# Attention: who subtracts the low parts of the weights, and who scales the softmax

## The chip, the cores and the metric

The kernel runs on one core of a Trainium2 chip. The metric is the device time of one execution in microseconds (us). The core has TensorE for matmuls and transposes (PE in the rows, and PEld for its loads of the stationary operand), VectorE (DVE), ScalarE (ACT), GpSimd (POOL) and SyncE (SP), which issues most of the DMA transfers. Each engine works through its own instructions in order and waits on semaphores for the others.

## The reference

A trunk of two layers over 512 positions of width 1024: sliding-window attention, a feed-forward network, a gated DeltaNet, and a second feed-forward network. Only the attention is touched. It projects to 16 query heads and 4 key and value heads of 64 dimensions, normalises and rotates queries and keys, and takes for each block of 128 queries a softmax over this and the previous block of keys, with a learned sink:

```python
qkv = u @ w_in
q = partial_rope(rms_norm(q, q_gain), cos, sin)
k = partial_rope(rms_norm(k, k_gain), cos, sin)
scores = jnp.einsum("bnqhgd,bnkhd->bnhgqk", qb, kb) * (hd ** -0.5)
scores = jnp.where(mask[None, :, None, None], scores, jnp.finfo(jnp.float32).min)
probs = jax.nn.softmax(jnp.concatenate([scores, sink], axis=-1), axis=-1)[..., :-1]
out = jnp.einsum("bnhgqk,bnkhd->bnqhgd", probs.astype(vb.dtype), vb)
return out.reshape(B, S, ATTN_Q_DIM) @ w_out
```

## The kernel before

Every large matmul is made of three: a float32 operand is split into a high part, rounded to the type that TensorE takes fast, and a low part, the rest. `mm3` (lines 146 to 150) multiplies high by high, high by low and low by high into the same accumulator. `weight` (line 128) prepares a weight tile: SyncE loads `raw` (line 136), ScalarE casts it to `whi` (line 137), VectorE subtracts to `wlo` (line 138). The three tiles have three buffers each, so a tile's cast has to wait until TensorE is through with the tile three before it.

The attention (`attn`) has three parts that run into each other.

- The projection is six blocks, c = 0 to 5, of 256 columns: keys, two blocks of queries, values, two blocks of queries. A block uses two weight tiles of 128x1024, one for k = 0 to 3 and one for k = 4 to 7, each k taking 256 of the 1024 columns. From c = 1 on, the loop runs over four position blocks t outside and over k inside, three matmuls for each. In the projection the high part of the input is the first operand, so of the three matmuls line 148 and line 150 read `whi`, and line 149 reads `wlo`. After each block `post` normalises and rotates (`qk_norm`, a long series of small VectorE instructions that contains the Newton steps of `rsqrt`, lines 163 to 169), ScalarE and VectorE each copy half of the keys to `kd` (line 420), and TensorE transposes them.
- Two lanes, i = 0 and 1, take two key heads each through the softmax. `attn_scores` forms the scores of four query heads (line 515), VectorE adds the mask and takes the maximum (line 518), ScalarE forms the exponentials and their sums (line 524), VectorE takes the reciprocal (line 526), and line 528 scales the four: heads 0 and 2 on VectorE, 1 and 3 on GpSimd. `attn_turn` transposes the scaled weights on TensorE (line 537) and copies them back (`pT`, line 539), and `attn_values` multiplies by the values (line 546). There are 16 such softmaxes, of 128 columns for the first block of a lane and of 256 for the others.
- The output projection has two halves of eight tiles, each with a weight tile of 128x512 and twelve matmuls of 512 columns. Its first half needs the first lane, its second half the second lane. So the second lane runs beside the first half, and the second half begins when the last softmax of the second lane has been through TensorE.

The program's text sets a coarse order: generators are pumped between groups of matmuls. A scheduler then fixes the order of instructions on each engine before the run, by its own estimates of when each can start. So moving work from one engine to another can also reorder what stays.

GpSimd does nothing else in this stage. Its next work is in the DeltaNet.

Of the kernel before, what the change touches and what calls it, by code (L numbers as in the profile page):

```python
# [10 lines left out]
F32 = mybir.dt.float32  # L11
# [3 lines left out]
ALU = mybir.AluOpType  # L15
# [55 lines left out]
class Builder:  # L71
# [53 lines left out]
        return self.cols[:, i:i + 1]  # L125


    def weight(self, src, cols=1024, parts=1):
        nc = self.nc
        raw = self.wp.tile([P, 1024], F32, tag="raw", name="raw")  # L130
        hi = self.wp.tile([P, 1024], F32R, tag="whi", name="whi")
        lo = self.wp.tile([P, 1024], F32R, tag="wlo", name="wlo")
        w = cols // parts
        for i in range(parts):
            s = slice(i * w, (i + 1) * w)
            nc.sync.dma_start(raw[:, s], src[:, s])
            nc.scalar.copy(hi[:, s], raw[:, s])  # L137
            nc.vector.tensor_tensor(lo[:, s], raw[:, s], hi[:, s].bitcast(F32), op=ALU.subtract)  # L138
        return hi, lo

    def split(self, src, hi, lo):
# [254 lines left out]
    def attn(self, h, after):  # L396
        nc = self.nc
        u = self.u
        at = self.big
        stack = ExitStack()  # L400
        self.ax = stack.enter_context(self.tc.tile_pool(name="ax", bufs=2))
        kT = [at.tile([P, T], F32, tag="a2", name="a2") for _ in range(4)]
        v = self.ax.tile([P, NB, 256], F32, tag="v", name="v", bufs=1)
        qT, ao, ready = {}, {}, set()

        def post(c, pss):
            while self.bc is None:
                yield 0.5
            if c == 3:
                for t in range(NB):  # L410
                    nc.scalar.activation(v[:, t], pss[t // 2][:, (t % 2) * 256:(t % 2) * 256 + 256], AF.Copy, scale=self.rc[:, t:t + 1])
                ready.add("v")
                return
            qn = self.ax.tile([P, 2, 8, 64], F32, tag="qn", name="qn", bufs=2)
            self.qk_norm(pss, qn, 64 if c == 0 else 0)
            qv = qn.rearrange("p i (t h) d -> p (i t) h d", h=4)
            if c == 0:
                kd = self.ax.tile([P, NB, 4, 2, 64], F32, tag="kd", name="kd", bufs=1)
                for i in range(2):
                    (nc.scalar.copy if i else nc.vector.tensor_copy)(kd[:, :, :, i], qv)  # L420
            yield 8 if c == 0 else 6
            dst = kT if c == 0 else [at.tile([P, T], F32, tag="a2", name="a2") for _ in range(2)]
            for i, x in enumerate(dst):
                pt = self.psum()
                for t in range(NB):
                    a = kd[:, t, i] if c == 0 else qv[:, t, 2 * i:2 * i + 2]
                    nc.tensor.transpose(pt[:, t * P:(t + 1) * P], a.rearrange("p h d -> p (h d)"), self.ident)
                nc.scalar.activation(x, pt, AF.Copy, scale=self.gcol[:, (c == 0):(c == 0) + 1])
                yield 1
            if c:  # L430
                g = c - 1 if c < 3 else c - 2
                qT[g] = dst
                ready.add(g)

        def lane(i):


            sc, pT = {}, {}
            for x in range(NB + 2):
                if x >= 2:  # L440
                    while "v" not in ready:
                        yield 0.5
                    n = x - 2
                    if n == 0:
                        ao[i] = [(self.a2(), self.a2()) for _ in range(4)]
                    po = self.psum()
                    both = [pT.pop((n, j)) for j in range(2)]
                    for b in range(len(both[0])):
                        for j in range(2):
                            self.attn_values(n, 2 * i + j, both[j], v, po, b)  # L450
                    for g in range(4):
                        s = slice(n * P, (n + 1) * P)
                        hi, lo = ao[i][g]
                        self.split(po[:, g * P:(g + 1) * P], hi[:, s], lo[:, s])
                    if n == NB - 1:
                        ready.add(("o", i))
                        return
                    yield 1
                for j in range(2):
                    kv = 2 * i + j  # L460
                    if x < NB:
                        while kv not in ready:
                            yield 0.5
                        sc[x, j] = self.attn_scores(x, kv, qT[kv], kT[kv])
                        yield 0.5
                    if 1 <= x < NB + 1:
                        pT[x - 1, j] = self.attn_turn(x - 1, sc.pop((x - 1, j)))
                        yield 0.5

        def lanes():  # L470
            for i in range(2):
                yield from lane(i)

        for c in range(6):
            W = self.W0 if c == 0 else [self.weight(self.ins["win"][c, kp]) for kp in range(2)]
            pss = [self.psum() for _ in range(2 if c else NB)]
            order = [(t, k) for t in range(NB) for k in range(KT)] if c else [(t, k) for k in range(KT) for t in range(NB)]
            for i, (t, k) in enumerate(order):
                ts = slice(t * P, (t + 1) * P)
                ps = pss[t // 2][:, (t % 2) * 256:(t % 2) * 256 + 256] if c else pss[t][:, :256]  # L480
                hi, lo = W[k // 4]
                s = slice(k % 4 * 256, k % 4 * 256 + 256)
                self.mm3(ps, (u[k][0][:, ts], u[k][1][:, ts]), (hi[:, s], lo[:, s]), k == 0, k == KT - 1)
                if i % 2 == 1:
                    self.pump(0.5)
            self.spawn(post(c, pss))
            if c == 0:
                self.attn_setup()
            if c == 1:
                self.spawn(lanes())  # L490
        for i in range(2):
            self.until(lambda: ("o", i) in ready)
            for m in range(KT):
                hi, lo = self.weight(self.ins["wout"][i, m], 512)
                ps = self.psum()
                self.dense(ps, hi, lo, ao[i], 4, grain=1)
                nc.vector.tensor_tensor(h[m], h[m], ps, op=ALU.add)
                if i:
                    after(m, h[m])
        stack.close()  # L500

    def attn_scores(self, n, kv, qT, kT):
        nc = self.nc
        W = P if n == 0 else 2 * P
        k0 = 0 if n == 0 else (n - 1) * P
        sc = self.ax.tile([P, 4, 2 * P], F32, tag="sc", name="sc", bufs=4)
        mx = self.small.tile([P, 4], F32, tag="mx", name="mx")
        nm = self.small.tile([P, 4], F32, tag="nm", name="nm")
        sm = self.small.tile([P, 4], F32, tag="sm", name="sm")
        es = self.small.tile([P, 4], F32, tag="es", name="es")  # L510
        sink = self.rows[:, 128 + kv * 4:128 + kv * 4 + 4]
        pss = [self.psum(), self.psum()]
        for g in range(4):
            r = slice((g % 2) * 64, (g % 2) * 64 + 64)
            nc.tensor.matmul(pss[g % 2][:, (g // 2) * W:(g // 2) * W + W], qT[g // 2][r, n * P:(n + 1) * P],  # L515
                             kT[r, k0:k0 + W], start=True, stop=True)
        for g in range(4):
            nc.vector.tensor_tensor_reduce(sc[:, g, :W], pss[g % 2][:, (g // 2) * W:(g // 2) * W + W],
                                           self.band[:, 2 * P - W:], 1.0, sink[:, g:g + 1], ALU.add, ALU.max, mx[:, g:g + 1])
        nc.vector.tensor_scalar(nm, mx, -1.0, None, op0=ALU.mult)  # L520
        nc.vector.tensor_tensor(es, sink, mx, op=ALU.subtract)
        nc.scalar.activation(es, es, AF.Exp)
        for g in range(4):
            nc.scalar.activation(sc[:, g, :W], sc[:, g, :W], AF.Exp, bias=nm[:, g:g + 1], accum_out=sm[:, g:g + 1])  # L524
        nc.vector.tensor_tensor(sm, sm, es, op=ALU.add)
        nc.vector.reciprocal(sm, sm)  # L526
        for g in range(4):
            (nc.gpsimd if g % 2 else nc.vector).tensor_scalar(sc[:, g, :W], sc[:, g, :W], sm[:, g:g + 1], None, op0=ALU.mult)  # L528
        return sc

    def attn_turn(self, n, sc):
# [647 lines left out]
```

## Time and profile before

| | |
|---|---|
| median of 3 runs | 1482.37 us (1481.43 to 1483.67) |
| profiled execution | 1481.57 us, its span 1479.8 us |
| TensorE busy | 1466.2 us, 99% of the span |
| VectorE busy | 913.7 us, 62% |
| ScalarE busy | 636.3 us, 43% |
| GpSimd busy | 104.7 us, 7% |
| attention stage | about 0 to 184 us of the span |

The span runs from the first to the last instruction. A matmul's row gives a modelled end, so a full TensorE is not one at its peak, and what counts is where it waited, for how long, and for whom. A row of the timeline that ends in x2 or more joins instructions that follow each other directly.

### The profile page before, as it was taken

How to read it: one execution, taken by the hardware profiler on the slowest of the kernel's cores; microseconds unless marked ns; L12 is line 12 of the kernel's file. 1: busy time of each engine (PE TensorE's matmuls, PEld its weight loads, DVE VectorE, ACT ScalarE, POOL GpSimd, SP SyncE). 2: the span in 40 equal slices, each digit the busy share in tenths (PEclk: the TensorE clock that was granted, in tenths of full speed). 3: DMA queues.
4: the chain of work that ended last, by engine and by line, in shares of the span. 5: the costliest groups of instructions: out<-in, count | busy, mean ns of one | idle time of the engine just before them, and what ended most of it. 6: DMA issues, size and time to landing. Idle time of an engine off the chain costs nothing.

```text
span 1479.8 us, 20837 instructions
## 1 busy us (share of the span) xinstructions
PE 1466.2 (99%) x7972; PEld 1216.8 (82%) x7972; DVE 913.7 (62%) x1772; ACT 636.3 (43%) x1206; POOL 104.7 (7%) x141
## 2 busy tenths in 40 slices
PE   8999999999999999999999999999999999999998
PEld 8976688888888888878888888888888888888887
DVE  8778765446635556765685667767685535644552
ACT  6666643223313334667534454454453313322331
POOL 0122100000000000000112222230000000000000
PEclk9999999999999999999999999999999999999999
DMA  5201222222222233356866445453222222222231
GB/s 188 72 19 60 82 98 100 100 100 100 86 99 100 100 121 121 118 174 229 278 230 210 150 142 174 154 162 122 73 101 98 100 100 100 88 98 100 100 106 65
DMA packets 70940, 178.14 MB, mean 120 GB/s; under 512 B 17208, under 2 KB 23352, under 8 KB 70584
## 3 DMA queue, kind: packets, MB, share of 16 engines
q1 hardware_dynamic: 61128, 158.70, 32.1%
q10 hardware_dynamic: 7920, 16.27, 2.9%
q0 software_dynamic: 1792, 1.84, 0.7%
q8 instruction: 63, 1.03, 0.3%
q14 instruction: 37, 0.30, 0.1%
HBM read 150.46 MB, written 26.31 MB: 119 GB/s over the span
## 4 chain that ended last, share of the span: by engine, by line
PE 93%; DVE 3%; DMA 3%; ACT 1%; issue 1%; POOL 0%; SPq 0%; ACTq 0%; DVEq 0%; POOLq 0%
PE ps L148 27%; PE ps L149 27%; PE ps L150 27%; PE ps L574 1%; PE ps L1061 1%; PE ps L1074 1%; PE ps L515 1%; PE ps L546 1%; PE ps L1067 1%; PE ps L1056 1%; PE ps L1052 1%; DVE wlo L138 1%; ACT sc L524 1%; PE ps L537 1%; DMA vd<-t 1%; PE ps L1027 1%
## 5 line engine op out<-in xcount | busy, mean ns | idle before, releaser
L148 PE MATMUL ps<-a,whi 128*128 128x512 f32 x1736 | 688.9, 397 | 0.4 <-ACT a L143 0.4
L150 PE MATMUL ps<-a,wlo 128*128 128x512 f32 x1736 | 677.1, 390 | 0.0
L149 PE MATMUL ps<-a,whi 128*128 128x512 f32 x1736 | 676.9, 390 | 0.0
L137 ACT CAST whi<-raw 128x1024 fp32r<-128x1024 f32 (+1 forms) x239 | 242.4, 1015 | 434.1 <-PE ps L149 389.9
L148 PEld LDWEIGHTS ps<-a,whi 128*128 128x128 f32 x1736 | 325.4, 188 | 70.5 <-issue 2.5
L150 PEld LDWEIGHTS ps<-a,wlo 128*128 128x128 f32 x1736 | 325.2, 187 | 69.3
L149 PEld LDWEIGHTS ps<-a,whi 128*128 128x128 f32 x1736 | 325.8, 188 | 64.0 <-DVE a L144 0.2
L138 DVE TENSOR_TENSOR wlo<-raw,whi 128x1024 fp32r<-128x1024 f32 (+1 forms) x239 | 282.1, 1181 | 68.1 <-ACT whi L137 67.6
L258 DVE TENSOR_TENSOR h<-h,ps 128x512 f32<-128x512 f32 x48 | 33.0, 688 | 148.5 <-PE ps L150 148.5
L243 DVE TENSOR_TENSOR t<-ps,rbc 128x512 f32<-128x512 f32 x48 | 33.2, 691 | 109.3 <-PE ps L150 103.9
L249 DVE TENSOR_TENSOR t<-ps,rbc 128x512 f32<-128x512 f32 x48 | 33.2, 691 | 86.4 <-PE ps L150 86.3
L247 ACT ACTIVATE t<-t 128x512 f32<-128x512 f32 x48 | 30.4, 632 | 97.8 <-DVE t L246 97.8
L148 PE MATMUL ps<-whi,a 128*128 128x256 f32 x192 | 56.9, 298 | 1.2 <-ACT a L192 1.2
L149 PE MATMUL ps<-wlo,a 128*128 128x256 f32 x192 | 54.0, 283 | 1.2 <-DVE wlo L138 1.2
L150 PE MATMUL ps<-whi,a 128*128 128x256 f32 x192 | 53.1, 283 | 0.0
L954 POOL MEMSET TT<- 128x1024 f32 x8 | 7.7, 958 | 562.8 <-DMA Xd<-kd 554.9
L143 ACT CAST a<-t 128x512 fp32r<-128x512 f32 x48 | 29.9, 624 | 32.6 <-DVE t L250 32.6
L148 PEld LDWEIGHTS ps<-whi,a 128*128 128x128 f32 x192 | 36.6, 191 | 7.6 <-issue 4.9
L566 DVE SCALAR_TENSOR_TENSOR t<-ps,cols,t 128x511 f32<-128x511 f32 (+2 forms) x48 | 35.7, 744 | 7.1 <-ACT t L564 6.5
L244 ACT ACTIVATE t<-t,cols 128x512 f32<-128x512 f32 x48 | 38.9, 810 | 0.0
L528 POOL TENSOR_SCALAR sc<-sc,sm 128x256 f32<-128x256 f32 (+1 forms) x32 | 28.9, 913 | 128.2 <-DVE sm L526 65.1
L149 PEld LDWEIGHTS ps<-wlo,a 128*128 128x128 f32 x192 | 36.6, 191 | 1.4 <-DVE wlo L138 1.4
(252 smaller groups left out, 1472.5 us busy)
## 6 DMA issues: line engine op xcount, KB each, us to landing
raw<-in_up SPq DMA_DIRECT2D x96, 512.0 KB, 3.2
raw<-in_down SPq DMA_DIRECT2D x48, 512.0 KB, 3.2
raw<-in_gin SPq DMA_DIRECT2D x48, 512.0 KB, 3.6
raw<-in_gout SPq DMA_DIRECT2D x16, 512.0 KB, 3.5
raw<-in_win SPq DMA_DIRECT2D x10, 512.0 KB, 3.1
raw<-in_wout SPq DMA_DIRECT2D x16, 256.0 KB, 2.7
zd<-t ACTq DMA_DIRECT2D x16, 256.0 KB, 3.0
Dd<-D ACTq DMA_DIRECT2D x8, 512.0 KB, 2.7
```

What stands on the lines that cost most here:

```text
L137: nc.scalar.copy(hi[:, s], raw[:, s])
L138: nc.vector.tensor_tensor(lo[:, s], raw[:, s], hi[:, s].bitcast(F32), op=ALU.subtract)
L143: nc.scalar.copy(hi, src)
L148: mm(ps, w[0], x[0], start=first, stop=False)
L149: mm(ps, w[0], x[1], start=False, stop=False)
L150: mm(ps, w[1], x[0], start=False, stop=last)
L243: nc.vector.tensor_tensor(g, gu[0], self.bc, op=ALU.mult)
L244: nc.scalar.activation(y, g, AF.Identity, bias=self.col(C_FB + l * 24 + j), scale=self.col(cw + 2))
L247: nc.scalar.activation(y, y, AF.Silu)
L249: nc.vector.tensor_tensor(t, gu[1], self.bc, op=ALU.mult)
L258: nc.vector.tensor_tensor(h[m], h[m], ps, op=ALU.add)
L566: nc.vector.scalar_tensor_tensor(dst[:, i:], g[:, :T - i], self.col(cw + 3 - i), dst[:, i:], op0=ALU.mult, op1=ALU.add)
```

## The change

In the attention, but for its first projection block, GpSimd subtracts the low parts of the weights. Tiles of 128x1024 are subtracted in two halves, tiles of 128x512 in one. All four scalings of a softmax go to VectorE. The other stages call `weight` as before.

```diff
-    def weight(self, src, cols=1024, parts=1):
+    def weight(self, src, cols=1024, parts=1, pool=0):
...
             nc.scalar.copy(hi[:, s], raw[:, s])
-            nc.vector.tensor_tensor(lo[:, s], raw[:, s], hi[:, s].bitcast(F32), op=ALU.subtract)
+            if not pool:
+                nc.vector.tensor_tensor(lo[:, s], raw[:, s], hi[:, s].bitcast(F32), op=ALU.subtract)
+        for i in range(pool):
+            s = slice(i * cols // pool, (i + 1) * cols // pool)
+            nc.gpsimd.tensor_tensor(lo[:, s], raw[:, s], hi[:, s].bitcast(F32), op=ALU.subtract)
         return hi, lo
...
-            W = self.W0 if c == 0 else [self.weight(self.ins["win"][c, kp]) for kp in range(2)]
+            W = self.W0 if c == 0 else [self.weight(self.ins["win"][c, kp], pool=2) for kp in range(2)]
...
-                hi, lo = self.weight(self.ins["wout"][i, m], 512)
+                hi, lo = self.weight(self.ins["wout"][i, m], 512, pool=1)
...
         for g in range(4):
-            (nc.gpsimd if g % 2 else nc.vector).tensor_scalar(sc[:, g, :W], sc[:, g, :W], sm[:, g:g + 1], None, op0=ALU.mult)
+            nc.vector.tensor_scalar(sc[:, g, :W], sc[:, g, :W], sm[:, g:g + 1], None, op0=ALU.mult)
```

Lines behind `weight` have numbers higher by four in the changed kernel: 528 becomes 532, 420 becomes 424, and so on. The order of instructions moves at three places that the prediction speaks of.

ScalarE, between the first key block and the second weight of c = 2. Of the names, `rbc` holds the normalising factors, `sn` and `cc` the sines and cosines, `ea` a constant of the DeltaNet, `t` a scratch tile of squares; the first CAST is the weight in question. Before:

```order
L213 COPY rbc<-ps 128x512
L620 ACTIVATE ea<-grow 128x16
L367 ACTIVATE t_585<-ps 128x512
L333 ACT_TABLE_LOAD
L333 ACTIVATE sn<-ra 128x4x8
L332 ACTIVATE cc<-ra 128x4x8 x2
L137 CAST whi<-raw 128x1024
L367 ACTIVATE t_588<-ps 128x512
L137 CAST whi<-raw 128x1024
L420 COPY kd<-qn 128x16x64
```

In the changed kernel:

```order
L217 COPY rbc<-ps 128x512
L337 ACT_TABLE_LOAD
L337 ACTIVATE sn<-ra 128x4x8
L371 ACTIVATE t_589<-ps 128x512
L336 ACTIVATE cc<-ra 128x4x8 x2
L603 CAST selr<-sel 128x16
L624 ACT_TABLE_LOAD
L624 ACTIVATE ea<-grow 128x16
L424 COPY kd<-qn 128x16x64
L137 CAST whi<-raw 128x1024
L371 ACTIVATE t_592<-ps 128x512
L137 CAST whi<-raw 128x1024
```

The cast of the second weight of c = 2 now comes behind the copy of `kd`, and behind a second table load, which before stood later, ahead of the first exponential.

VectorE, at the end of the second lane, from the maxima of the last softmax to its scaling (ISA is the instruction of line 518, `nm` the negative maxima, `es` the sinks, `sm` the sums). Before:

```order
L518 ISA sc,mx<-ps,band,rows 128x256
L518 ISA mx 128x1
L528 TENSOR_SCALAR sc<-sc,sm 128x256 x2
L520 TENSOR_SCALAR nm<-mx 128x4
L521 TENSOR_TENSOR es<-rows,mx 128x4
L138 TENSOR_TENSOR wlo<-raw,whi 128x512
L525 TENSOR_TENSOR sm<-sm,es 128x4
L144 TENSOR_TENSOR a_1871<-ps,a_1870 128x128
L526 RECIPROCAL sm<-sm 128x4
L528 TENSOR_SCALAR sc<-sc,sm 128x256 x2
```

In the changed kernel:

```order
L522 ISA sc,mx<-ps,band,rows 128x256
L522 ISA mx 128x1
L532 TENSOR_SCALAR sc<-sc,sm 128x256 x4
L524 TENSOR_SCALAR nm<-mx 128x4
L525 TENSOR_TENSOR es<-rows,mx 128x4
L529 TENSOR_TENSOR sm<-sm,es 128x4
L148 TENSOR_TENSOR a_1881<-ps,a_1880 128x128
L530 RECIPROCAL sm<-sm 128x4
L532 TENSOR_SCALAR sc<-sc,sm 128x256 x4
```

Both scalings have four instructions in place of two, at the same places; the subtraction is gone.

TensorE, at the same place: the transposes of the scaled weights (`sc` with the identity) and the products with the values. Before:

```order
L537 MATMUL ps<-ident,sc 128x128 x8
L546 MATMUL ps<-pT,v 64x512 x4
L537 MATMUL ps<-ident,sc 128x128 x16
L546 MATMUL ps<-pT,v 64x512 x4
L148 MATMUL ps<-a_1870,whi 128x512 x2
```

In the changed kernel:

```order
L541 MATMUL ps<-ident,sc 128x128 x8
L550 MATMUL ps<-pT,v 64x512 x4
L541 MATMUL ps<-ident,sc 128x128 x10
L550 MATMUL ps<-pT,v 64x512
L541 MATMUL ps<-ident,sc 128x128 x6
L550 MATMUL ps<-pT,v 64x512 x3
L152 MATMUL ps<-a_1880,whi 128x512 x2
```

One product with the values has moved in among the last transposes.

## Rows read from the trace of the kernel before

**Rows 1.** Busy time by stretch: us, PE, PEld, DVE, ACT, POOL, PEclk, DMA, GB/s

```profile
148.00:162.00 14.00, 11.65 (x51) 5.69 (x50) 7.10 (x29) 9.20 (x31) 3.73 (x4) 0.88 0.08 22
...
184.00:1479.00 1295.00, 1289.58 (x6834) 1073.43 (x6832) 772.74 (x1222) 518.44 (x900) 75.57 (x105) 1.00 0.38 126
```

**Rows 2.** Waits of TensorE, 0 to 200 us: us in total, times, longest

```profile
PE ps L537 <- DVE sc L528: 1.3, 1, 1.3
...
PE ps L537 <- POOL sc L528: 0.9, 2, 0.5
```

**Rows 3.** Instructions of one line: ns min/median/max, first and last start, forms

```profile
L528 DVE TENSOR_SCALAR sc<-sc,sm x32: 278/352/570, 59.1 to 155.8; 128x256 f32<-128x256 f32 x24, 128x128 f32<-128x128 f32 x8
...
L1008 POOL TENSOR_TENSOR qd<-a,qd x16: 1002/1016/2083, 725.1 to 1005.2; 128x384 f32<-128x384 f32 x16
...
L979 POOL TENSOR_TENSOR kd<-kd,ck x16: 828/834/1552, 727.1 to 993.9; 128x384 f32<-128x384 f32 x16
```

**Rows 4.** Timeline, VectorE and GpSimd: start us, us, engine line, operation [idle before]

```profile
38.98 0.18 DVE L163 TENSOR_SCALAR nt<-ss 128x16 int32<-128x16 int32 x1
...
40.03 0.17 DVE L167 TENSOR_TENSOR nt<-ss 128x16 f32<-128x16 f32 x1
...
92.54 1.91 POOL L528 TENSOR_SCALAR sc<-sc,sm 128x256 f32<-128x256 f32 x2 [6.28 <-DVE ss L373]
...
93.14 0.16 DVE L163 TENSOR_SCALAR nt<-ss 128x16 int32<-128x16 int32 x1
...
94.48 0.17 DVE L167 TENSOR_TENSOR nt<-ss 128x16 f32<-128x16 f32 x1
```

**Rows 5.** Timeline of ScalarE, 17 to 38 us, casts of c = 1 and 2

```profile
17.25 1.05 ACT L137 CAST whi<-raw 128x1024 fp32r<-128x1024 f32 x1 [0.22 <-DMA raw<-in_win]
...
20.41 1.04 ACT L137 CAST whi<-raw 128x1024 fp32r<-128x1024 f32 x1
...
30.77 1.28 ACT L333 ACT_TABLE_LOAD   x1
...
33.92 1.05 ACT L137 CAST whi<-raw 128x1024 fp32r<-128x1024 f32 x1 [1.17 <-issue]
...
36.75 1.05 ACT L420 COPY kd<-qn 128x1024 f32<-128x1024 f32 x1
```

**Rows 6.** Timeline of VectorE, 20 to 37 us, subtractions and what follows them

```profile
20.50 1.22 DVE L138 TENSOR_TENSOR wlo<-raw,whi 128x1024 fp32r<-128x1024 f32 x1
21.63 0.15 DVE L168 TENSOR_TENSOR nt<-nt,rv 128x4 f32<-128x4 f32 x1
...
35.03 1.22 DVE L138 TENSOR_TENSOR wlo<-raw,whi 128x1024 fp32r<-128x1024 f32 x1
36.16 0.28 DVE L394 TENSOR_TENSOR qn<-qn,rt 128x128 f32<-128x128 f32 x1
```

**Rows 7.** Timeline of TensorE, 20 to 38 us, first uses of low parts

```profile
21.77 0.39 PE L149 MATMUL ps<-wlo,a 128*128 128x256 f32 x1 [1.20 <-DVE wlo L138]
...
24.15 1.16 PE L210 MATMUL ps<-ident,rc 128*128 128x128 f32 x8 [0.69 <-DVE rc L169]
...
36.67 0.28 PE L149 MATMUL ps<-wlo,a 128*128 128x256 f32 x1
...
37.39 0.28 PE L149 MATMUL ps<-wlo,a 128*128 128x256 f32 x1
```

**Rows 8.** Timeline, 131 to 162 us: scalings, one subtraction, start of the second half

```profile
131.65 0.61 DVE L528 TENSOR_SCALAR sc<-sc,sm 128x256 f32<-128x256 f32 x2
...
145.37 0.68 DVE L138 TENSOR_TENSOR wlo<-raw,whi 128x512 fp32r<-128x512 f32 x1
...
155.49 0.83 DVE L528 TENSOR_SCALAR sc<-sc,sm 128x256 f32<-128x256 f32 x2
...
155.65 1.88 POOL L528 TENSOR_SCALAR sc<-sc,sm 128x256 f32<-128x256 f32 x2 [2.31 <-ACT pT L539]
...
161.75 0.73 PE L148 MATMUL ps<-a,whi 128*128 128x512 f32 x2 [0.35 <-ACT a L143]
```

## The prediction

> **What bounds the kernel now.** I read the busy time by stretch first. From 184 us to the end TensorE works 1289.6 of 1295 us, and that stretch holds none of the edited lines, so the edit can only move it in time, not shorten it [rows 1]. The attention stage before it is just as full, except between 148 and 162 us, where TensorE is busy 11.65 of 14 us and its granted clock falls to 0.88 (full is 2.4 GHz, the lower level 1.2) [rows 1]. Then I read what TensorE waited for in the first 200 us. Of what the edit touches there are three things: 1.3 us and 0.9 us for the scaled weights of the softmax (line 528, by VectorE and by GpSimd) [rows 2], one wait of 1.20 us for the low part of a projection weight at 21.77 us, and one of 0.69 us for `rc`, which comes late from the same VectorE queue, at 24.15 us [rows 7]. Together 4.1 us of 1480: the edit is about stalls of this size, gained or made. VectorE's and GpSimd's total busy times are beside the point.
>
> **What it changes.** 26 low parts (10 of 128x1024, 16 of 128x512) leave VectorE and become 36 subtractions of 128x512 on GpSimd; 32 scalings leave GpSimd for VectorE, so every softmax has four there in a row instead of two and two. The instruction order of TensorE hardly changes. SyncE issues one more weight load ahead of two small tables, which no matmul awaits. No DMA is added, and GpSimd has no DMA to issue in this stage.
>
> *Price of one GpSimd subtraction.* No row has a 128x512 one. The nearest, 128x384 multiplications of two operands, take 0.834 us (one operand repeated) and 1.016 us (output strided) [rows 3]: times 4/3 that is 1.11 and 1.35. Two scalings, together 512 elements, take 1.88 us [rows 8]. Bounds 1.11 and 1.88; I take 1.2, since the subtraction is dense throughout and so nearest to the two multiplications.
>
> *Price of one scaling on VectorE.* Two take 0.61 us when GpSimd's first comes late, 0.83 us when it runs between them [rows 8]. One takes 0.352 in the median [rows 3], so in the undisturbed pair the second follows after 0.26, and four take 0.35 + 3 x 0.26 = 1.13 us, instead of GpSimd's 1.88 to the end of the last.
>
> *GpSimd beside VectorE.* Under a pair of GpSimd scalings (92.54 for 1.91 us) VectorE goes from its line 163 at 93.14 to the second line 167 at 94.48, 1.34 us; the same steps without GpSimd go from 38.98 to 40.03, 1.05 us [rows 4]. I take 0.29 us lost per 1.34 us of overlap.
>
> *Step 1, projection block c = 1 (20 to 26 us).* The cast of the first weight ends at 18.30 [rows 5], GpSimd is idle, and both halves are ready at 19.5 and 20.7. TensorE was due for the first at 20.57 (21.77 less 1.20), so the 1.20 goes; `rc` comes earlier, since a 1.13 us subtraction (20.50 to 21.63) is out of its way [rows 6], and its matmuls now stand eleven matmuls later in TensorE's order: the 0.69 goes too. Late next is the second weight: its cast ends at 21.45 [rows 5], the halves at 22.7 and 23.9. TensorE spends 0.12 us a matmul (36.67 to 37.39 is six) [rows 7]; it reaches k = 4 after 12, at 22.0, and waits 0.7; then k = 6 after six more, at 23.4, and waits 0.5. Net -1.89 + 1.2 = **-0.7** (-0.9 at 1.11; +1.2 at 1.88, where the first weight's second half is late as well).
>
> *Step 2, block c = 2 (33 to 38 us).* Here the order on ScalarE matters. The second weight's cast, before at 33.92, now stands behind the second table load (1.28 us) and the copy of `kd` (1.05 us) [rows 5], and that copy waits for `qn`. Before, `qn` was done at 36.44 with four subtractions ahead of it (first and last shown), 1.13 us each [rows 6]; without them 31.9. From about 20.5 to 26.3 GpSimd works beside that chain, and 5.8/1.34 x 0.29 gives back 1.25: 33.2. The table load is done by then (the rows end it at 32.05, and it moves behind a second, 1.28 us: 33.3). Copy to 34.3, cast to 35.3, halves at 36.5 and 37.7. TensorE, now 0.7 early, is due for k = 4 at 36.0 and k = 6 at 36.7: it stalls about 0.5 twice, and the second half at 37.7 against 37.39 before [rows 7] sets the stage **+0.3** later than before, in place of step 1's gain. Bounds for steps 1 and 2 together: -0.9 (no slowing, 1.11) to +2.6 (1.88, slowing to match). In the later blocks and the output projection the cast comes microseconds ahead of need, and one subtraction per output tile (12 matmuls) is hidden.
>
> *Step 3, first lane (98 us).* One of the two GpSimd waits [rows 2] goes, since four VectorE scalings are done before GpSimd's second would be; the two make 0.9, so I take half: **-0.45** (or 0).
>
> *Step 4, end of the second lane (148 to 162 us).* TensorE has nothing left but the last two softmaxes, so their latency is on the path. The next-to-last scaling delays the last `nm` by four times 0.26, 1.05, instead of the pair's 0.83, but the subtraction of 0.68 us at 145.37 is gone [rows 8]; I call that even. The last scaling started at 155.49 and ended on GpSimd at 157.53 (155.65 plus 1.88), when the last transposes could begin; on VectorE it ends at 156.6 [rows 8]. That is 0.9, and one value matmul now stands among the transposes, 0.1 or more: **-1.0**. Bounds: -2.1 (all of TensorE's waits here: 1.3 and half of 0.9 [rows 2], and 0.35 [rows 8]) to +0.3 (nothing but the later `nm`).
>
> Sum: 0.3 - 0.45 - 1.0 = **-1.2 us**, bounds -3.5 to +2.9. Against the profiled execution of 1481.57 us (span 1479.8) that is 1480.4; the median of the runs shown, 1482.37, lies 0.8 higher: **1481.2 us**. A measurement of this kernel tells 0.2%, or 3 us, from no change.
>
> **Rivals.** *Faster:* the slowing on VectorE doesn't show and the subtraction is near 1.11, so step 1 keeps its 0.9, and the last lane loses all its waits: -3.5, 1478.9. For it speaks that the chain is otherwise free; against it that no stage but the last has more than 1 us to give. *Slower, by the lock:* each GpSimd subtraction stops VectorE's small operations on SBUF until it ends. Then the chain to `qn` stands still from 21.5 to 26.3 (four halves): `qn` at 36.7, copy 37.8, cast 38.8, second half 41.3: +3.9; step 3 gives nothing and step 4 loses a subtraction's 1.2 us to one scaling, +0.2: about +4, 1486.4. It decides once more than about 3.7 of those 4.8 us are lost. Against it: under the GpSimd pair VectorE did get through six steps in 1.34 us [rows 4]. The Trainium skill's page "SBUF — State Buffer", section "Who interferes with whom", states that rule: an exclusive lock, where the second to issue fully blocks. The trace shows 0.29 us of it per 1.34 us, so I leave it one chance in nine. *No effect:* the subtraction at 1.88 eats the gains of steps 3 and 4: 2.6 - 1.45 = +1.1, 1483.5. That the change doesn't do what it says is excluded by the order: all 36 subtractions stand on GpSimd, no scaling does.
>
> **Chances.** Forecast 0.50 and no effect 0.23, both within 0.2%: 0.73. Faster 0.16. Slower by the lock 0.11. The range leaves out half of the faster rival and the lock: 1478.7 to 1484.8.
>
> **What would show it.** Line 142 on GpSimd at 1.1 to 1.4 us each; TensorE's wait at 21.8 us gone and two short ones for `wlo` near 22 and 23; the cast of c = 2 at 34 us and `wlo` waits near 36 to 37; no wait for line 532 near 98; the output projection's second half starting 1 to 2 us before 161.75. Subtractions over 1.9 us, or VectorE standing still under them, would make the prediction wrong upwards; no `wlo` waits at all, downwards.

## The result: 14 us slower

The changed kernel takes 1497.33 us (median of 4, 1496.63 to 1498.22), the one before 1483.02 (1481.43 to 1484.90): a ratio of 1.0091, 95% interval 1.0078 to 1.0103. That lies above the predicted range, and it is a loss where a gain of 1.2 us was forecast. A view by windows of the changed kernel (columns: stretch; its length and PE's busy time; PEld, DVE, ACT, POOL; granted clock; DMA share; GB/s):

```profile
25.00:30.00 5.00, 1.96 (x10) 1.75 (x9) 5.00 (x35) 0.00 (x0) 1.89 (x2) 0.75 0.65 214
30.00:35.00 5.00, 5.00 (x27) 5.00 (x27) 5.00 (x43) 2.10 (x3) 0.00 (x0) 0.57 0.01 1
...
162.00:184.00 22.00, 18.14 (x74) 10.53 (x73) 10.11 (x35) 13.05 (x39) 3.87 (x3) 0.92 0.10 25
184.00:1495.00 1311.00, 1304.86 (x6898) 1085.25 (x6896) 786.18 (x1239) 528.98 (x916) 79.90 (x108) 1.00 0.39 126
```

The last row answers to the second of [rows 1]: from 184 us on TensorE is as full as it was. What is new lies ahead of it: TensorE idles for 3 of 5 us at 25 us and for almost 4 between 162 and 184 us, in the tail of the second lane. What TensorE waited for in the first 220 us (the total, how often, the longest):

```profile
PE ps L214 <- DVE rc L173: 3.0, 1, 3.0
PE ps L550 <- ACT pT L543: 2.9, 3, 1.3
PE ps L541 <- DVE sc L532: 2.1, 1, 2.1
PE ps L431 <- DVE qn L398: 1.9, 2, 1.7
...
PE ps L153 <- POOL wlo L142: 1.3, 3, 0.8
```

Against [rows 2] the waits for GpSimd's scalings are gone, and so is the 1.20 us for the first weight [rows 7]. In their place TensorE waits for **VectorE**, from which the change took work away, and 2.9 us for `pT`, ScalarE's copies of the transposed weights (0.2 before). For GpSimd's subtractions themselves it waits 1.3 us in all.

**Where the 14 us lie.** The same matmul of line 148 (152 in the changed kernel) can be counted off in both traces. At these marks TensorE has done the same number of each kind of matmul in every kernel here, so the difference in the start of that matmul is the loss so far. The table gives what each stretch added, in us, in the changed kernel and in the eleven experiments; stretches are named by the times of the kernel before. "Start" holds how the first loads happened to arrive in the profiled execution, and differs by up to 2.7 us between kernels, for which I found no cause in the code, so a total here is not the ratio of the runs. From 167 to 600 us no kernel gains or loses more than 0.6 us, the changed one nothing; behind that the profiled executions differ by another -0.6 to +2.5 us.

| kernel | start, 0 to 20 | c = 1, to 32 | c = 2, to 42 | to 69 | first lane, to 116 | second `qn`, to 122 | second lane, to 167 | ratio to before (95%) |
|---|---|---|---|---|---|---|---|---|
| changed | +0.3 | **+5.2** | +0.4 | +0.6 | **+2.4** | **+2.1** | **+3.7** | 1.0091 (1.0078 to 1.0103) |
| e1_scale | +2.6 | +0.7 | 0.0 | 0.0 | -0.6 | -0.1 | -0.9 | 0.9991 (0.9982 to 1.0000) |
| e2_sub | -0.1 | +3.8 | +0.4 | +0.6 | +2.4 | +4.8 | -0.6 | 1.0077 (1.0062 to 1.0092) |
| e3_win | +0.4 | +4.7 | +0.4 | +0.6 | +1.3 | -0.1 | -0.8 | 1.0035 (1.0022 to 1.0048) |
| e7_wout | +0.5 | +0.5 | 0.0 | 0.0 | +1.2 | +4.5 | +1.0 | 1.0042 (1.0027 to 1.0058) |
| e4_c2 | +0.4 | +4.9 | +0.4 | +0.3 | +2.4 | +2.1 | +2.5 | 1.0090 (1.0073 to 1.0106) |
| e4_c3 | +0.5 | 0.0 | 0.0 | +0.2 | +2.4 | +2.0 | +2.4 | 1.0059 (1.0044 to 1.0074) |
| e5_form | +0.8 | -0.6 | +0.7 | 0.0 | +1.6 | -0.2 | -0.4 | 1.0004 (0.9995 to 1.0014) |
| e6_small | +0.3 | +1.3 | +4.9 | +0.6 | +3.5 | +1.4 | +0.9 | 1.0077 (1.0059 to 1.0096) |
| e9_two | +0.6 | +6.1 | +1.0 | +2.1 | +0.3 | +4.2 | +2.0 | 1.0102 (1.0086 to 1.0119) |
| e9_one | +0.8 | +1.4 | +1.8 | +0.6 | -0.4 | +1.0 | -0.9 | 1.0019 (1.0010 to 1.0029) |
| e10_best | +0.4 | -0.3 | +0.4 | 0.0 | -0.7 | -0.1 | -0.9 | 0.9997 (0.9988 to 1.0005) |

The last two columns hold something beside the edits, the granted clock of the profiled execution. In the kernel before it falls to 0.72 at 156 to 162 us, in the tail of the second lane. In e3_win, which leaves that lane as it was, it is 1.00 there (162 to 169 us), and the stretch is 0.8 us shorter: a -0.8 or -0.9 in this column can come from the clock alone. At the second `qn` the clock falls to 0.83 in e2_sub, e7_wout and e9_two, which have 4.2 to 4.8 there; in the changed kernel it stays at 1.00.

**What the trace shows of the cause.** First GpSimd's side: all 36 subtractions as one group of the lines view, then its first six as rows of the timeline (start, duration).

```profile
L142 POOL TENSOR_TENSOR wlo<-raw,whi 128x512 fp32r<-128x512 f32 x36 | 46.1, 1298 | 145.6 <-ACT whi L137 145.1 <-DVE ra L315 0.5
```

```profile
18.75 2.61 POOL L142 TENSOR_TENSOR wlo<-raw,whi 128x512 fp32r<-128x512 f32 x2 [18.30 <-ACT whi L137]
21.87 5.02 POOL L142 TENSOR_TENSOR wlo<-raw,whi 128x512 fp32r<-128x512 f32 x4 [0.51 <-DVE ra L315]
```

VectorE in the same microseconds:

```profile
20.19 1.20 DVE L289 TENSOR_SCALAR ra<-ra 128x32 f32<-128x32 f32 x1
...
21.90 1.28 DVE L289 TENSOR_SCALAR ra<-ra 128x32 f32<-128x32 f32 x1
23.09 0.15 DVE L171 TENSOR_TENSOR nt<-rc 128x4 f32<-128x4 f32 x1
23.21 1.22 DVE L290 TENSOR_SCALAR ra<-ra 128x32 f32<-128x32 f32 x1
24.35 0.15 DVE L172 TENSOR_TENSOR nt<-nt,rv 128x4 f32<-128x4 f32 x1
24.42 0.67 DVE L375 TENSOR_REDUCE ss<-t 128x8 f32<-128x512 f32 x1
25.02 0.64 DVE L173 SCALAR_TENSOR_TENSOR rc<-nt,rc 128x4 f32<-128x4 f32 x1
...
25.68 1.24 DVE L289 TENSOR_SCALAR ra<-ra 128x32 f32<-128x32 f32 x1
...
26.91 0.17 DVE L289 TENSOR_SCALAR ra<-ra 128x32 f32<-128x32 f32 x1
```

Line 289 on 128x32 takes 0.17 us when GpSimd is done (26.91) and 1.20 to 1.28 under a subtraction, ending where the subtraction ends. One or two small instructions slip through where one subtraction gives way to the next (23.09, 24.35), then the next is held for another whole one. In the first 215 us 21 VectorE instructions are stretched, each against the usual time of its line and shape, by 19.3 us together; in the kernel before, 11 by 2.3. Not all are held: a reduction (24.42) runs its usual time, and so do the instructions that read PSUM in these rows of GpSimd and VectorE (lines 148 and 522 take 0.28 and 0.45 elsewhere):

```profile
94.57 2.53 POOL L142 TENSOR_TENSOR wlo<-raw,whi 128x512 fp32r<-128x512 f32 x2 [21.03 <-ACT whi L137]
```

```profile
94.69 0.29 DVE L148 TENSOR_TENSOR a<-ps,a 128x128 fp32r<-128x128 f32 x1 [1.01 <-ACT a L147]
94.90 0.47 DVE L522 CUSTOM_DVE_ANT_0 sc<-ps,band,rows 128x256 f32<-128x256 f32 x1
```

So what is held are `TENSOR_SCALAR` on SBUF and instructions with two SBUF operands. The Trainium skill's page "SBUF — State Buffer", section "Who interferes with whom", names the same kinds, excepts reductions on this chip, and says that the second to issue is blocked until the first ends; the trace agrees, with up to 1.1 us lost each time.

TensorE's view of c = 1. The bracket is its idle time and what ended it:

```profile
23.20 0.38 PE L153 MATMUL ps<-wlo,a 128*128 128x256 f32 x1 [0.80 <-POOL wlo L142]
...
24.45 0.38 PE L153 MATMUL ps<-wlo,a 128*128 128x256 f32 x1 [0.28 <-POOL wlo L142]
...
28.35 2.08 PE L214 MATMUL ps<-ident,rc 128*128 128x128 f32 x8 [3.04 <-DVE rc L173]
...
30.43 0.41 PE L153 MATMUL ps<-wlo,a 128*128 128x256 f32 x1
30.65 0.41 PE L154 MATMUL ps<-whi,a 128*128 128x256 f32 x1
```

`rc` is the end of a chain of 13 small VectorE instructions (line 208 and lines 167 to 173, the last three of them three times), and the sines and cosines share its queue; held five times between 20 and 27 us, it lets TensorE wait 3.04 us, where it was 0.69 [rows 7]. Behind it matmuls start every 0.22 us (30.43 to 30.65) instead of 0.12: the granted clock is 0.57 from 30 to 35 us, which costs another 1.9, and the eight matmuls of line 214 themselves take 2.08 us instead of 1.16.

### The profile page after: what moved, and what is told of

Its sections match the earlier page's. It is cut to its first block, busy times and chain, and to the rows that moved or that the text cites. A ratio compares the mean times of both kernels' runs of the same rounds, so it can differ in the third digit from the quotient of the medians.

```text
span 1495.8 us, 20815 instructions
## 1 busy us (share of the span) xinstructions
PE 1474.1 (99%) x7972; PEld 1219.5 (82%) x7972; DVE 919.8 (61%) x1778; ACT 635.2 (42%) x1206; POOL 122.3 (8%) x145
## 3 DMA queue, kind: packets, MB, share of 16 engines
q8 instruction: 63, 1.03, 0.3%
## 4 chain that ended last, share of the span: by engine, by line
PE 89%; DVE 5%; DMA 3%; ACT 2%; issue 1%; POOL 0%; ACTq 0%; SPq 0%; DVEq 0%; POOLq 0%
PE ps L152 26%; PE ps L154 26%; PE ps L153 26%; PE ps L578 1%; ACT sc L528 1%; PE ps L1065 1%; PE ps L1078 1%; PE ps L550 1%; DMA z<-zd 1%; PE ps L1071 1%; PE ps L1060 1%; DMA h<-in_xT 1%; PE ps L1056 1%; PE ps L1025 1%; DVE sc L522 1%
## 5 line engine op out<-in xcount | busy, mean ns | idle before, releaser
L139 DVE TENSOR_TENSOR wlo<-raw,whi 128x1024 fp32r<-128x1024 f32 (+1 forms) x213 | 258.3, 1213 | 59.8 <-ACT whi L137 59.5
L142 POOL TENSOR_TENSOR wlo<-raw,whi 128x512 fp32r<-128x512 f32 x36 | 46.1, 1298 | 145.6 <-ACT whi L137 145.1
```

Of the source, the lines that this page charges most:

```text
L142: nc.gpsimd.tensor_tensor(lo[:, s], raw[:, s], hi[:, s].bitcast(F32), op=ALU.subtract)
```

## The experiments

All times are against the kernel before on the same chip; the ratios and the losses by stretch stand in the table above.

### The two halves of the change apart

Scalings alone:

```diff
-            W = ... self.weight(self.ins["win"][c, kp], pool=2) ...
+            W = ... self.weight(self.ins["win"][c, kp], pool=0) ...
-                hi, lo = self.weight(self.ins["wout"][i, m], 512, pool=1)
+                hi, lo = self.weight(self.ins["wout"][i, m], 512, pool=0)
```

> Only the scalings go to VectorE; every subtraction stays on VectorE, so GpSimd has no work in this stage. Theory (GpSimd's subtraction holds up VectorE): nothing is held, TensorE keeps its full clock at 25 to 35 us, and the time is the one before within 2 us, 1481 to 1485. Rival (four scalings in a row on VectorE put the work of the lanes in a worse order; that is what the 2.8 us at 88 to 97 us and most of the 3.7 us at the end of the second lane are): 1486 to 1490.

1481.56 us against 1483.42. Nothing is held, and the gain forecast for the first lane is there, -0.6. The -0.9 at the end of the second lane is not shown to be a gain of the scalings, since e3_win has -0.8 with the scalings as before. Rows of VectorE and TensorE at that end: the last scaling takes 1.14 us, TensorE waits 0.55 for it instead of the 1.3 of [rows 2], and then 0.40 for a `pT`.

```profile
158.13 1.14 DVE L532 TENSOR_SCALAR sc<-sc,sm 128x256 f32<-128x256 f32 x4
```

```profile
158.54 0.44 PE L541 MATMUL ps<-ident,sc 128*128 128x128 f32 x2 [0.55 <-DVE sc L532]
```

The profiled execution shows a low clock at 25 to 30 us, against the expectation (0.68), behind a late start. The rival that blamed four scalings in a row falls.

Subtractions alone:

```diff
-            nc.vector.tensor_scalar(sc[:, g, :W], ...)
+            (nc.gpsimd if g % 2 else nc.vector).tensor_scalar(sc[:, g, :W], ...)
```

> Only the subtractions go to GpSimd; the scalings stay two and two. Theory: all of the loss comes from the subtractions, so about the changed kernel's time, 1494 to 1499. Rival (the scalings make the losses in the lanes, 2.8 and about 3 us): 1489 to 1492.

1495.73 us: the loss comes with the subtractions. Divided between projection and output projection (both with the scalings as before):

```diff
e3_win
-                hi, lo = self.weight(self.ins["wout"][i, m], 512, pool=1)
+                hi, lo = self.weight(self.ins["wout"][i, m], 512, pool=0)
e7_wout
-            W = ... self.weight(self.ins["win"][c, kp], pool=2) ...
+            W = ... self.weight(self.ins["win"][c, kp], pool=0) ...
```

> Only the projection's subtractions go to GpSimd; those of the output projection and the scalings are as before the change. Theory: block c = 1 loses its 5.6 us (3.7 of waiting, 1.9 of clock), and of what is lost later (2.8 at 88 to 97, 2.1 at 124 to 133, 3.7 at the end of the second lane) what lies beside the output projection, the last 3.7, comes back: 1491 to 1495. Rival (the loss comes from four scalings and from the output projection's subtractions; the early one is made good later): 1483 to 1488.

> Only the output projection's subtractions go to GpSimd; the projection and the scalings are as before. Theory: nothing is lost before 110 us; beside the lanes the subtractions hold scalings and the second queries' qn, and the loss is what the run with all subtractions had over that with the projection's alone, 6.9 us: 1488 to 1491. Rival (an output tile's subtraction is hidden by its twelve matmuls): 1482 to 1485.

1488.79 and 1490.23 us. By the ratios that is +5.2 and +6.2, and the sum is the +11.4 of both together. The projection's part was expected larger, and 1488.79 lies between the ranges of the theory and of its rival: the loss at the second `qn` isn't the projection's, since by then the subtractions are those of the output projection. An output tile's subtraction is indeed hidden from TensorE, which waits for none of them in e7_wout; the run loses 6 us all the same, 4.5 of them at the second `qn`, for which TensorE waits 2.9 us.

### Taking the early blocks out

```diff
-            W = ... self.weight(self.ins["win"][c, kp], pool=2) ...
+            W = ... self.weight(self.ins["win"][c, kp], pool=2 * (c > 1)) ...
```

> The changed kernel, but block c = 1 is subtracted on VectorE as before; GpSimd begins with c = 2. Theory: with no GpSimd instruction beside the chain to rc, TensorE's 3.0 us wait and the low clock behind it (1.9 us) go: 1491 to 1493. Rival (what came late in c = 1 is due to the new order of ScalarE's and TensorE's instructions, not to GpSimd): 1495 to 1498.

1496.48 us, ratio 1.0090: next to nothing comes back. That is the rival's number, but not for its reason. The rows of GpSimd, VectorE and TensorE tell why: with c = 1 out of the way, GpSimd took the first weight of c = 2 at 23.11, beside the same chain.

```profile
23.11 2.51 POOL L142 TENSOR_TENSOR wlo<-raw,whi 128x512 fp32r<-128x512 f32 x2 [22.65 <-DVE ra L289]
```

```profile
23.16 1.26 DVE L290 TENSOR_SCALAR ra<-ra 128x32 f32<-128x32 f32 x1
...
24.41 1.25 DVE L290 TENSOR_SCALAR ra<-ra 128x32 f32<-128x32 f32 x1
```

```profile
26.67 2.08 PE L214 MATMUL ps<-ident,rc 128*128 128x128 f32 x8 [1.89 <-DVE rc L173]
```

Two instructions held are enough for 1.9 us of waiting instead of 0.69; the first weight's own 1.20 us is back as well. Most of the rest of the 4.9 goes with a low clock, 0.50 at 25 to 30 us. It is 0.50 at 22.5 to 24.5 already, ahead of the wait for `rc`, so the trace doesn't show that the hold brought it down. One block further:

```diff
+            W = ... self.weight(self.ins["win"][c, kp], pool=2 * (c > 2)) ...
```

> As the last run, but c = 1 and c = 2 are both subtracted on VectorE; GpSimd begins with c = 3. In the run from c = 2 on GpSimd took the first weight of c = 2 at 23.1 to 25.6 us, still beside the chain to rc, and held two instructions there. Theory: now nothing is held before 40 us, the 5.2 us lost by 30 us go and the losses in the lanes (about 7.5) stay: 1489 to 1492. Rival (the early loss comes from the instruction order that the edit leaves behind): 1495 to 1498.

1492.34 us, 0.3 above the theory's range. The loss in c = 1 is gone altogether, with the clock at 1.00 from 25 to 35 us; the lanes' losses are those of the changed kernel except for the last stretch, where the clock is 1.00 too (162 to 184 us; 0.92 in the changed kernel). So the early 5 us, waits and clock together, hang on GpSimd's working beside the chain to `rc`, as the theory has it.

### One operand in place of two

```diff
-            nc.gpsimd.tensor_tensor(lo[:, s], raw[:, s], hi[:, s].bitcast(F32), op=ALU.subtract)
+            nc.gpsimd.tensor_scalar(lo[:, s], raw[:, s], 1e-4, None, op0=ALU.mult)
```

> As the changed kernel, but GpSimd's instruction reads one tile instead of two: it scales raw by 1e-4, so the low parts are not the true ones and only the time counts. Theory (what holds VectorE is GpSimd's form with two SBUF operands; its scalings of one operand, 0.95 us each in these traces, cost a VectorE instruction only about 0.2 us): no VectorE instruction is stretched by more than 0.3 us. The GpSimd instruction itself is longer, about 1.9 us by two scalings, so TensorE waits more for wlo in c = 1 and 2: 1483 to 1489. Rival (any GpSimd instruction on these tiles holds VectorE until it ends): stretches of 1 to 1.9 us and 1498 or more.

1484.61 us against 1484.31. GpSimd has 36 instructions on the same tiles, each longer than before. TensorE and VectorE have the same instructions in the same order as in the changed kernel (on ScalarE four change places, on SyncE three loads). And all but 0.6 us of the loss is gone, so the new orders on these two engines don't make it. A group of GpSimd's lines and the VectorE row that is stretched as the others are:

```profile
L142 POOL TENSOR_SCALAR wlo<-raw 128x512 fp32r<-128x512 f32 x36 | 54.7, 1520 | 123.9 <-PE ps L154 66.7 <-issue 37.9 <-DMA raw<-in_win 17.3
```

```profile
23.05 0.59 DVE L289 TENSOR_SCALAR ra<-ra 128x32 f32<-128x32 f32 x1
...
23.63 0.17 DVE L289 TENSOR_SCALAR ra<-ra 128x32 f32<-128x32 f32 x1
```

Of a GpSimd instruction of 1.52 us VectorE loses 0.35 to 0.46 once in most cases (more than the 0.3 expected), and then runs freely. One term doesn't go: the first lane still loses 1.6 of its 2.4 us.

### Shorter GpSimd instructions

```diff
-            W = ... pool=2) ...
+            W = ... pool=8) ...
-                hi, lo = self.weight(self.ins["wout"][i, m], 512, pool=1)
+                hi, lo = self.weight(self.ins["wout"][i, m], 512, pool=4)
```

> The changed kernel with each GpSimd subtraction cut into four of 128x128. Theory (a held VectorE instruction waits until the GpSimd instruction ends, then one passes): stretches of at most 0.5 us instead of 1.1, the chain to rc gets through four times as often, the wait for rc and the clock's fall shrink; 1485 to 1491. Rival (it is the amount of GpSimd's traffic that slows VectorE, not the length of one instruction): 1496 or more, with the overhead of 108 further instructions.

1496.17 us, what the rival expected, but not for its reason. GpSimd's group, and VectorE under it:

```profile
L142 POOL TENSOR_TENSOR wlo<-raw,whi 128x128 fp32r<-128x128 f32 x144 | 63.2, 474 | 127.3 <-ACT whi L137 127.3
```

```profile
23.07 0.43 DVE L289 TENSOR_SCALAR ra<-ra 128x32 f32<-128x32 f32 x1
23.43 0.15 DVE L171 TENSOR_TENSOR nt<-rc 128x4 f32<-128x4 f32 x1
23.50 0.44 DVE L289 TENSOR_SCALAR ra<-ra 128x32 f32<-128x32 f32 x1
```

VectorE is held until the end of one piece, then one or two instructions pass, as the theory says: the wait for `rc` falls to 0.85 us and c = 1 loses 1.3 instead of 5.2. But 16 pieces in a row take 6.7 us where four whole subtractions take 5.0 (both from 40 us on), and 71 instructions are held by 0.26 instead of 21 by 0.92, which is 18.7 us and so nearly as much as before. The chain to the first `qn` is still held: the `kd` copy starts at 37.04 (35.26 in e5_form), the cast behind it comes late, TensorE waits 0.80 us for that cast at 39.09 and for its low parts after it, the granted clock falls to 0.76 at 40 to 45 us, and c = 2 loses 4.9. Cutting up GpSimd's instruction moves the loss, and hardly lessens it.

### The hold by itself

To the kernel of e1_scale 36 GpSimd instructions are added that nobody waits for; TensorE, VectorE, ScalarE and SyncE have the same instructions in the same order as there.

```diff
             nc.vector.tensor_tensor(lo[:, s], raw[:, s], hi[:, s].bitcast(F32), op=ALU.subtract)
+        if pool: spare = self.ax.tile([P, 384], mybir.dt.bfloat16, tag="spare", ...)
+        for i in range(pool):
+            s = slice(i * cols // pool, i * cols // pool + 384)
e9_two
+            nc.gpsimd.tensor_tensor(spare, raw[:, s], hi[:, s].bitcast(F32), op=ALU.subtract)
e9_one
+            nc.gpsimd.tensor_scalar(spare, raw[:, s], 1e-4, None, op0=ALU.mult)
```

> The kernel with only the scalings moved, to which 36 GpSimd subtractions of 128x384 are added where the change has its 36; each reads both raw and whi and writes a spare tile that nobody reads, while VectorE still makes the true low parts. TensorE, VectorE, ScalarE and SyncE have the same instructions in the same order as in the run with the scalings alone (1481.6). Theory: GpSimd's two-operand instruction by itself holds VectorE, about 0.9 us each time, and TensorE waits for it in c = 1, for qn and at the end of the second lane: 1486 to 1492. Rival (the loss is in the new orders of the engines, and a GpSimd instruction that nobody waits for costs nothing): 1481 to 1484.

> The same, but the 36 added GpSimd instructions read raw alone (a scaling by 1e-4 into the spare tile). Theory: with one operand a VectorE instruction is put off by 0.2 to 0.5 us, as in the earlier run of this form, and not until the end: 1481 to 1484. Rival (any GpSimd instruction on these tiles does it): as the two-operand run, 1486 or more.

With two operands 1497.63 us, with one 1486.56, against 1483.28 (and 1481.56 without them, in the other call). In VectorE and TensorE of the first:

```profile
26.29 0.97 DVE L172 TENSOR_TENSOR nt<-nt,rv 128x4 f32<-128x4 f32 x1
```

```profile
28.37 2.08 PE L214 MATMUL ps<-ident,rc 128*128 128x128 f32 x8 [2.77 <-DVE rc L173]
```

and of the second:

```profile
24.01 0.49 DVE L171 TENSOR_TENSOR nt<-rc 128x4 f32<-128x4 f32 x1
```

No new order is left to blame, and nothing waits for GpSimd but the release of `raw` and `whi`, which have three buffers each: the instruction by itself costs 16.5 us, by the ratios to the kernel before (1.0102 here, 0.9991 in e1_scale). The time came out almost 6 us above the top of the expectation. VectorE's own subtractions are here too and collide with GpSimd's (at 137.76 us one takes 1.50 us instead of 0.69); how much of the 6 us that makes was not tried. The one-operand instruction is about as long, 1.28 us in the mean against 1.25, and costs 4.2 us by the same reckoning: each puts off VectorE by about 0.3, which the dense chains of c = 1 and c = 2 pass on (+1.4 and +1.8). That is more than the theory expected, and 1486.56 lies in the rival's range; but it is a quarter of what the two-operand instruction costs in the same places. The two differ in their operation as well, a subtraction and a scaling, and which of the two differences counts was not tried.

### A better version

```diff
-            nc.gpsimd.tensor_tensor(lo[:, s], raw[:, s], hi[:, s].bitcast(F32), op=ALU.subtract)
+            nc.vector.tensor_tensor(lo[:, s], raw[:, s], hi[:, s].bitcast(F32), op=ALU.subtract)
-            W = ... pool=2) ...
+            W = ... pool=4 * (c == 1)) ...
-                hi, lo = self.weight(self.ins["wout"][i, m], 512, pool=1)
+                hi, lo = self.weight(self.ins["wout"][i, m], 512, pool=0)
```

> No GpSimd work in this stage, all scalings on VectorE, and the two low parts of c = 1 subtracted on VectorE in quarters of 128x256, so that TensorE can begin with the first quarter. Hope: of the 1.2 us that TensorE waits for the first weight of c = 1 up to 0.8 goes, beside the gains at 98 us and at the end of the second lane: 1479.5 to 1482, against 1483 to 1484 before. Rival (the quarters put off rc and the later chain by as much): 1481.5 to 1484.

1482.88 us against 1483.28, ratio 0.9997 (0.9988 to 1.0005): the same, and in the rival's range, not in the hoped-for one. The first weight's wait falls from 1.20 to 0.40 us in the trace, the one for `rc` grows from 0.69 to 1.0. The scalings alone (0.9991, up to 1.0000) are as good. No version here is measurably faster than the kernel before.

## Why the prediction was wrong

**The step that failed** is "GpSimd beside VectorE": 0.29 us lost per 1.34 us of overlap. It was read from [rows 4], where GpSimd *scales*, and applied to its *subtraction*. Rows 4 are right for what they show: e5_form and e9_one measure 0.3 to 0.46 us per GpSimd instruction with one tensor operand. With two operands VectorE loses the rest of the running instruction, up to 1.1 us, each time an instruction of the kinds above comes up. From 20.5 to 26.3 us the prediction gave back 1.25 us; the five stretched rows above, 20.19 to 25.68, lose 1.0 + 1.1 + 1.05 + 0.5 + 1.1 = 4.7.

The trace of the kernel before had the answer, in the DeltaNet. There GpSimd multiplies two operands (line 1008), and a line 167 of VectorE comes up beside it, GpSimd first:

```profile
971.16 1.01 POOL L1008 TENSOR_TENSOR qd<-a,qd 128x384 f32<-128x384 f32 x1
```

```profile
971.18 1.03 DVE L167 TENSOR_TENSOR nt<-rs 128x8 f32<-128x8 f32 x1
```

It is the line that the prediction timed under a scaling; here it takes 1.03 us instead of 0.17 and ends with GpSimd's instruction. The prediction took its price of a subtraction from line 1008 [rows 3], but not its price for VectorE. The maximum in that row, 2083 ns against a median of 1016, was a sign of the same thing the other way round: that multiplication (838.24 us) stands beside a subtraction of VectorE.

**The rival "by the lock"** had the mechanism, and its condition was just met (3.7 of 4.8 us lost, by the four rows from 21.90 on), but it had the chain in front of the wrong wait: +3.9 at `qn` of c = 2. The wait that came was for `rc` in c = 1, which step 1 had down as gone. At c = 2 TensorE is already 5.5 us late, so the late cast (39.53) costs only 0.4; in e6_small, where it is not late, the same place costs 4.9. And it stopped at one scaling in the second lane. Its +4 us were less than a third of the way.

**Step 1.** The price of a subtraction held: 1.30 us, by [rows 3] 1.11 to 1.35. The first weight's wait went, and the two short ones for `wlo` came at 23.20 and 24.45 with 0.80 and 0.28 us (0.7 and 0.5 forecast). "The 0.69 goes too" was the error: it became 3.04.

**Step 2's last line**, that an output tile's subtraction is hidden, looked at who waits for GpSimd, not at whom GpSimd stops. The second `qn` is an example, GpSimd, VectorE and TensorE in turn:

```profile
125.10 2.69 POOL L142 TENSOR_TENSOR wlo<-raw,whi 128x512 fp32r<-128x512 f32 x2 [4.00 <-ACT whi L137]
```

```profile
126.36 1.58 DVE L394 TENSOR_TENSOR qn<-qn,rows 128x128 f32<-128x128 f32 x2
...
128.27 1.35 DVE L397 TENSOR_TENSOR qn<-qn,cc 128x128 f32<-128x128 f32 x1
```

```profile
130.01 0.44 PE L431 MATMUL ps<-ident,qn 128*128 128x128 f32 x2 [1.69 <-DVE qn L398]
```

**Steps 3 and 4.** For the scalings by themselves step 3 was right, -0.45 forecast and -0.6 measured in e1_scale, and four scalings take 1.14 us (1.13 forecast). Step 4's -1.0 looks right beside e1_scale's -0.9, but e3_win has -0.8 with the scalings as before and a clock that holds, so no more than 0.1 is shown for the scalings. The wait for the last one did shrink, from 1.30 to 0.55 us; what took that gain away was not followed up. With subtractions beside them both steps turn over. At the end of the second lane the next-to-last scaling stands ahead of the last `nm`, and GpSimd holds it:

```profile
164.70 1.27 POOL L142 TENSOR_TENSOR wlo<-raw,whi 128x512 fp32r<-128x512 f32 x1 [6.45 <-ACT whi L137]
```

```profile
165.10 1.81 DVE L532 TENSOR_SCALAR sc<-sc,sm 128x256 f32<-128x256 f32 x4
166.83 0.16 DVE L524 TENSOR_SCALAR nm<-mx 128x4 f32<-128x4 f32 x1
```

```profile
165.15 1.93 PE L550 MATMUL ps<-pT,v 128*64 128x512 f32 x6 [1.32 <-ACT pT L543]
...
170.20 0.44 PE L541 MATMUL ps<-ident,sc 128*128 128x128 f32 x2 [2.09 <-DVE sc L532]
...
176.33 0.74 PE L152 MATMUL ps<-a,whi 128*128 128x512 f32 x2 [0.36 <-ACT a L147]
```

The scaling at 165.10 takes 1.81 instead of 1.14 us, `nm` and the exponentials come later by as much, and TensorE waits 2.09 us for the last scaling. Two scalings before it are held as well (146.55 us, 1.91; 156.77 us, 2.15), the exponentials and ScalarE's copies to `pT` come late behind them, and TensorE waits 0.97 us (153.68) and 1.32 us (165.15) for `pT`, where it waited 0.20 in all before, and 0.33 in e5_form, which has the same order and no long hold. These two waits are more of the 3.7 us than the last scaling's, which was 1.3 and 0.5 (VectorE, then GpSimd) before. The output projection's second half starts at 176.33, where [rows 8] had 161.75 and the prediction 1 to 2 us earlier.

**The first lane's 2.4 us** nobody had foreseen, and for the most part they are not a hold: GpSimd idles for the 21.03 us ahead of 94.57 (row above), and e5_form, where nothing is held for long, still has 1.6. e1_scale with VectorE's subtractions in place has -0.6, and e3_win and e7_wout, each with a part of the subtractions moved, 1.3 and 1.2. So they go with taking the subtractions off VectorE and with the new orders that follow from it; the two were not tried apart. The prediction had that TensorE's order hardly changes. In the trace TensorE waits 0.65 us for `pT`, and value matmuls that stood together are split up: two alone take as much as 1.07 us, while six in a row take 1.93.

```profile
87.89 1.07 PE L550 MATMUL ps<-pT,v 128*64 128x512 f32 x2
...
91.12 1.93 PE L550 MATMUL ps<-pT,v 128*64 128x512 f32 x6 [0.65 <-ACT pT L543]
```

How the 2.4 divide between wait, split matmuls and the rest was not tried.

**What stays open.** The five kernels with a long wait for `rc` have a low clock at 25 to 30 us (0.50 to 0.75 in the changed one, e2_sub, e3_win, e4_c2 and e9_two), and e4_c3 without it has 1.00. But in e4_c2 the clock falls ahead of that wait, and it falls without any hold there in e1_scale (0.68 at 25 to 30 us) and e7_wout (0.71 at 20 to 25). So how much of what the low clock costs in c = 1 is owed to the hold is not settled.

## What to carry to other kernels

Before an operation goes to GpSimd, ask what VectorE does in those microseconds: here GpSimd instructions with two SBUF operands stopped VectorE's `TENSOR_SCALAR`s and two-operand instructions until it ended, up to 1.1 us at a time, so "off the critical path" has to hold for VectorE's chains, not for GpSimd's result. A price for two engines side by side carries over only between instructions of the same form: rows of a one-operand GpSimd instruction said nothing of a two-operand one here, and rows of the right form stood elsewhere in the same trace. A direct test is cheap: add the instruction with a result that nobody reads, and see what the time does.

## What the runs showed of the hardware that was not expected

- The form of the GpSimd instruction decides how long VectorE is held: to its end, up to 1.1 us of 1.30, by a subtraction of two tiles; 0.35 to 0.46 of 1.52 by a scaling of one (128x512), about 0.3 of 1.28 (128x384). By the rule of the Trainium skill's page "SBUF — State Buffer", section "Who interferes with whom", either would block to the end; the one-operand runs differ from that, and the measurement decides. Why it is so, no run here shows.
- A GpSimd scaling of 128x512 by a constant into the rounded type takes longer (1.52 us) than the subtraction of two tiles into it (1.30).
- Sixteen GpSimd subtractions of 128x128 in a row take 6.7 us, four of 128x512 5.0: some 0.14 us for each instruction more (estimated from (6.7 - 5.0) / 12).
